# A gated FFN on one NeuronCore: the up projection by Strassen's seven block products, and the down projection as a phase of its own

## The chip, the cores and the metric

One Trainium2 chip, of which the kernel uses one core. A core has five engines that run their own instruction queues: TensorE (PE, matrix products into PSUM), VectorE (DVE), ScalarE (ACT), GpSimd (POOL) and SyncE (SP, which here issues every DMA). PSUM has eight banks, and a product tile of 128 rows by 512 f32 columns fills one of them. The metric is the device time of one execution in microseconds.

## The reference, cut to what matters

The kernel is one layer of a decoder: a mixer of four branches, and behind it a gated FFN with a short causal convolution. Only the FFN and its neighbours are touched here. The width is 1024, the sequence 1024 tokens, `D_FF` is 2816, and everything is f32.

```
h = rmsnorm(x, ffn_pre_g) * (1.0 + sc2) + sh2
u = causal_dwconv(h @ w_up, ffn_conv_w, ffn_conv_b)   # 1024 -> 5632, 3 taps
gate, val = split(u, 2)
y = (silu(gate) * val) @ w_down                       # 2816 -> 1024
x = x + g2 * rmsnorm(y, ffn_post_g)
```

(The body of the FFN is written out here in one piece.)

## The kernel before, in words

A product in nearly full f32 precision is made of three fast products. Each operand is split into a high part (the value cast to the rounded f32 type, "hi") and a low part (the value less the high part, "lo"), and PE multiplies hi by hi, hi by lo and lo by hi. `split_w` (L179 and below) does this for a weight tile of 128 by 1024: a DMA into a raw buffer (`wr`, two buffers), the cast on ACT (L184), the subtraction on POOL (L185).

Tokens are worked on in two halves of 512. The loop over eight token tiles `t` ahead of the FFN (from L957) does the output projection of the mixer (`yps`, L968), two RMS norms, and the transposes `h2t` (L989) that turn the normed tile to channels by tokens. ACT applies scale and shift (L991), and DVE makes hi and lo (`h2h`, `h2l`, L994 and L995) for each half.

The FFN works through 22 blocks `j` of 128 gate channels and the 128 value channels that belong to them. `up(j)` loads two weight tiles (gate and value), and for each makes 48 matmuls: two token halves, eight blocks of 128 input channels, three products (L1017). ACT and DVE do the convolution straight from PSUM (L1021, L1022, L1024), then silu, gate times value (L1028), and hi and lo of the activations (L1031, L1032), which stay in SBUF. `down` takes a group of two blocks, one group behind: for each of eight token tiles 12 matmuls per block into a PSUM tile (L1047), which DVE adds to an accumulator `ya` in SBUF (L1052). So up and down products alternate on PE all through the FFN. The last group is followed by the final norm (`rstd_of`, L249 to L255), the factor `grow1` on POOL (L1060), the sum with `x1l` (L1063) and the stores.

The order of the instructions on each engine is set by a scheduler that reorders the rows within the limits of data and buffers; it is not the order of the source.

Of the kernel before, what the change touches and what calls it, by code (L numbers as in the profile page):

```python
# [10 lines left out]
F32 = mybir.dt.float32  # L11
# [11 lines left out]
S = 1024  # L23
D = 1024
# [88 lines left out]
def tile_hybrid_block(ctx, tc, x, pos, ada, pk, cst, w_in, w_br, w_out, w_up, w_dn, out):  # L113
# [47 lines left out]
    sg_s = dram.tile([32, P, S], F32, name="sg_s")  # L161
    o_s = dram.tile([8, P, S], F32, name="o_s")
    x1_s = dram.tile([NT, P, D], F32, name="x1_s")
    QK = {}

    def qkslot(n, i):
# [90 lines left out]
    pss = ctx.enter_context(pool("pss", 2, PSUM))  # L257
# [6 lines left out]
    hi_pri = ExitStack()  # L264
    mrg = ExitStack()
    wox = ExitStack()
    h2H = [None] * 2
    h2L = [None] * 2
    with ExitStack() as mix:
        hp = mix.enter_context(pool("hp", 1))  # L270
        gx = mix.enter_context(ExitStack())
# [658 lines left out]
                        (G if br else V).tensor_tensor(out=accs[c], in0=accs[c], in1=sg, op=OP.add)  # L930


    big = ctx.enter_context(pool("big", 4))
    with pool("mg", 2) as mgp, pool("sms", 8) as sms, wox:
        wo = {}

# [14 lines left out]
        with pool("tmp", 7, side="right") as tmp, pool("grp", 1, side="right") as grp:  # L951
            for kp in range(4):
                load_wo(1, kp, obp, V if kp % 2 else G)
            grow0 = grp.tile([P, D], F32, name="grow0")
            spread_row(grow0, Gm, ptt, "t", tmp, "t")
            for t in range(NT):
# [25 lines left out]
                if t % 4 == 0:  # L982
                    h2H[half] = big.tile([P, NK, 512], F32R, name="h2h", tag="b")
                    h2L[half] = big.tile([P, NK, 512], F32R, name="h2l", tag="b")
                hf32 = jk.rearrange("p (a b) -> p a b", b=P)
# [7 lines left out]
                hd, ld = h2H[half][:, :, tl], h2L[half][:, :, tl]  # L993
                V.tensor_copy(hd, hf32)  # L994
                V.tensor_tensor(out=ld, in0=hf32, in1=hd.bitcast(F32), op=OP.subtract)  # L995


    psx.close()
    with pool("yac", 1) as yac, pool("act", 8) as actp, pool("wd", 6) as wdp, pool("ut", 5) as ut, \
            pool("sme", 8) as sme, pool("pd", 2, PSUM) as pd:  # L1000
        ya = [yac.tile([P, D], F32, name=f"ya{t}") for t in range(NT)]
        GRP = 2
        groups = [list(range(g, g + GRP)) for g in range(0, NF - 4, GRP)] + [[NF - 4], list(range(NF - 3, NF))]

        def up(j):
            us = []
            for v in range(2):
                m = j + v * NF
                hi, lo = split_w(w_up[m])
                ps = pss.tile([P, S], F32, name="ups", tag="s")  # L1010
                for hf in range(2):
                    n = 0
                    for k in range(NK):
                        ks = slice(k * P, (k + 1) * P)
                        xh, xl = h2H[hf][:, k, :], h2L[hf][:, k, :]
                        for a, b in ((hi, xh), (hi, xl), (lo, xh)):
                            PE.matmul(ps[:, hf * 512:hf * 512 + 512], a[:, ks], b, start=(n == 0), stop=(n == 23))  # L1017
                            n += 1
                u = ut.tile([P, S], F32, name="u", tag="u")
# [4 lines left out]
                V.scalar_tensor_tensor(out=u[:, 2:], in0=ps[:, 0:S - 2], scalar=w(0), in1=u[:, 2:],  # L1024
                                       op0=OP.mult, op1=OP.add)
# [3 lines left out]
            hi = actp.tile([P, S], F32R, name="ah", tag="a")  # L1029
            lo = actp.tile([P, S], F32R, name="al", tag="a")  # L1030
            A.copy(hi, us[0])  # L1031
            V.tensor_tensor(out=lo, in0=us[0], in1=hi.bitcast(F32), op=OP.subtract)  # L1032
            return hi, lo

        def down(gi, acts):
            ws = [split_w(w_dn[j], wdp) for j in groups[gi]]
            last = gi == len(groups) - 1
            for t in range(NT):
                tb = slice(t * P, (t + 1) * P)
                ps = pd.tile([P, D], F32, name="dps", tag="d")  # L1040
                n = 0
                tot = 3 * len(ws)
                for (ah, al), (wh, wl) in zip(acts, ws):
                    for a, b in ((ah, wh), (ah, wl), (al, wh)):
                        for hf in range(2):
                            cs = slice(hf * 512, hf * 512 + 512)
                            PE.matmul(ps[:, cs], a[:, tb], b[:, cs], start=(n == 0), stop=(n == tot - 1))  # L1047
                        n += 1
# [4 lines left out]
                if last:  # L1053
                    sm = sme.tile([P, 8], F32, name="sm4", tag="sm")
                    jk = ut.tile([P, D], F32, name="jk2", tag="u")
                    A.activation(jk, ya[t], AF.Square, accum_out=sm[:, 0:1])
                    rstd_of(sm[:, 0:1], sm)
                    x1 = ut.tile([P, D], F32, name="x1l", tag="u")
                    dma(x1, x1_s[t])
                    G.tensor_tensor(out=ya[t], in0=ya[t], in1=grow1, op=OP.mult)  # L1060
                    for hf in range(2):
                        cs = slice(hf * 512, hf * 512 + 512)
                        V.scalar_tensor_tensor(out=x1[:, cs], in0=ya[t][:, cs], scalar=sm[:, 3:4], in1=x1[:, cs],  # L1063
                                               op0=OP.mult, op1=OP.add)
                        dma(out[tb, cs], x1[:, cs])

        grow1 = yac.tile([P, D], F32, name="grow1")
        pend = None
        for gi in range(len(groups)):
            if gi == len(groups) - 1:  # L1070
                spread_row(grow1, Gf, pd, "d", ut, "u")
            acts = [up(j) for j in groups[gi]]
            if pend is not None:
                down(*pend)
            pend = (gi, acts)
        down(*pend)
    return dict(qk_s=qk_s, o_s=o_s, sg_s=sg_s, x1_s=x1_s, A2=A2, B2=B2)


# [68 lines left out]
```

## Time and profile before

| | |
|---|---|
| median of three runs | 2039.09 us (2036.22 to 2039.84) |
| profiled execution, its own time | 2032.69 us |
| its span | 2030.9 us |
| granted TensorE clock over the span | 0.962 |
| PE busy | 1855.4 us, 91% |
| DVE, ACT, POOL busy | 57%, 41%, 23% |
| up matmuls (L1017), three groups of 704 | 2112 |
| down matmuls (L1047), three groups of 352 | 1056 |

The span runs from the first to the last instruction of the profiled execution, and times inside it are counted from its start. The FFN takes its last 755 us: the first up matmul starts at 1275.48. A matmul's listed duration (about 390 ns) overlaps with the next one's; what one costs is the distance from start to start.

### The profile page before, as it was taken

How to read it: one execution, taken by the hardware profiler on the slowest of the kernel's cores; microseconds unless marked ns; L12 is line 12 of the kernel's file. 1: busy time of each engine (PE TensorE's matmuls, PEld its weight loads, DVE VectorE, ACT ScalarE, POOL GpSimd, SP SyncE). 2: the span in 40 equal slices, each digit the busy share in tenths (PEclk: the TensorE clock that was granted, in tenths of full speed). 3: DMA queues.
4: the chain of work that ended last, by engine and by line, in shares of the span. 5: the costliest groups of instructions: out<-in, count | busy, mean ns of one | idle time of the engine just before them, and what ended most of it. 6: DMA issues, size and time to landing. Idle time of an engine off the chain costs nothing. (4 is left out here: it accounts for less than half of the span.)

```text
span 2030.9 us, 22858 instructions
## 1 busy us (share of the span) xinstructions
PE 1855.4 (91%) x8792; PEld 1443.3 (71%) x8792; DVE 1154.4 (57%) x1731; ACT 829.5 (41%) x1458; POOL 472.9 (23%) x244
## 2 busy tenths in 40 slices
PE   6888877499999999899999899999999999999996
PEld 3655555376767776677787668788888888888875
DVE  6759999605899857685113765532343334433457
ACT  5556666236545645463222444333122212221122
POOL 0102145272111110011205610222122212222024
PEclk9988989699999999899999999999999999999999
DMA  8364423444514242513113632121111101111114
GB/s 312 94 165 151 174 84 93 126 92 104 187 57 125 78 129 69 147 42 115 62 63 129 225 122 83 63 73 42 32 63 58 47 32 52 62 52 42 32 62 145
DMA packets 61038, 197.30 MB, mean 97 GB/s; under 512 B 9153, under 2 KB 9281, under 8 KB 60929
## 3 DMA queue, kind: packets, MB, share of 16 engines
q1 hardware_dynamic: 60928, 195.84, 30.6%
q8 instruction: 69, 1.13, 0.2%
q14 instruction: 41, 0.33, 0.1%
HBM read 154.13 MB, written 41.68 MB: 96 GB/s over the span
## 5 line engine op out<-in xcount | busy, mean ns | idle before, releaser
L185 POOL TENSOR_TENSOR wlo<-wraw,whi 128x1024 fp32r<-128x1024 f32 x126 | 317.4, 2521 | 1384.2 <-ACT whi L184 1348.2
L365 PE MATMUL mm<-hH,whi 128*128 128x512 f32 x864 | 353.5, 409 | 49.6 <-ACT whi L184 31.5
L365 PE MATMUL mm<-hH,wlo 128*128 128x512 f32 x864 | 350.4, 406 | 3.7 <-POOL wlo L185 3.7
L365 PE MATMUL mm<-hL,whi 128*128 128x512 f32 x864 | 351.9, 407 | 0.9 <-DVE hL L321 0.9
L184 ACT CAST whi<-wraw 128x1024 fp32r<-128x1024 f32 x144 | 150.6, 1049 | 413.2 <-PE ups L1017 283.7
L1017 PE MATMUL ups<-h2h,whi 128*128 128x512 f32 x704 | 277.6, 395 | 1.3 <-DVE h2h L994 1.3
L1017 PE MATMUL ups<-h2l,whi 128*128 128x512 f32 x704 | 277.5, 394 | 0.5 <-DVE h2l L995 0.5
L1017 PE MATMUL ups<-h2h,wlo 128*128 128x512 f32 x704 | 274.5, 390 | 0.0
L1022 DVE SCALAR_TENSOR_TENSOR u<-ups,pkt,u 128x1023 f32<-128x1023 f32 x44 | 56.4, 1283 | 350.8 <-ACT u L1021 350.8
L365 PEld LDWEIGHTS mm<-hH,whi 128*128 128x128 f32 x864 | 166.6, 193 | 95.6 <-ACT whi L184 32.0
L365 PEld LDWEIGHTS mm<-hH,wlo 128*128 128x128 f32 x864 | 166.5, 193 | 41.4 <-POOL wlo L185 4.8
L365 PEld LDWEIGHTS mm<-hL,whi 128*128 128x128 f32 x864 | 167.2, 194 | 36.1 <-issue 2.6
L1017 PEld LDWEIGHTS ups<-h2h,whi 128*128 128x128 f32 x704 | 132.6, 188 | 32.3 <-DVE h2h L994 1.7
L1017 PEld LDWEIGHTS ups<-h2h,wlo 128*128 128x128 f32 x704 | 132.5, 188 | 29.8
L1017 PEld LDWEIGHTS ups<-h2l,whi 128*128 128x128 f32 x704 | 132.7, 189 | 28.2 <-DVE h2l L995 1.0
L1052 DVE TENSOR_TENSOR ya<-ya,dps 128x1024 f32<-128x1024 f32 x80 | 97.3, 1217 | 58.8 <-PE dps L1047 58.6
L605 DVE TENSOR_SCALAR_CACHE_REDUCE junkb<-key,cf 128x1024 bf16<-128x1024 uint16 (+3 forms) x124 | 117.3, 946 | 4.3
L1047 PE MATMUL dps<-whi,ah 128*128 128x512 f32 x352 | 109.4, 392 | 5.5 <-DVE ya L1052 5.5
L1047 PE MATMUL dps<-wlo,ah 128*128 128x512 f32 x352 | 108.6, 390 | 0.0
L1047 PE MATMUL dps<-whi,al 128*128 128x512 f32 x352 | 108.4, 389 | 0.0
L872 DVE SCALAR_TENSOR_TENSOR hc<-hpad,pkt,hc 128x1024 f32<-128x1024 f32 x60 | 84.2, 1408 | 0.0
L1047 PEld LDWEIGHTS dps<-whi,ah 128*128 128x128 f32 x352 | 65.4, 188 | 22.2 <-DVE ya L1052 8.9
(560 smaller groups left out, 2950.3 us busy)
## 6 DMA issues: line engine op xcount, KB each, us to landing
wraw<-in_w_in SPq DMA_DIRECT2D x54, 512.0 KB, 3.9
adaw<-in_ada SPq DMA_DIRECT2D x48, 512.0 KB, 5.9
wraw<-in_w_up SPq DMA_DIRECT2D x44, 512.0 KB, 3.3
sg_s<-gt SPq DMA_DIRECT2D x44, 256.0 KB, 2.6
sgl<-sg_s SPq DMA_DIRECT2D x22, 512.0 KB, 3.4
wraw<-in_w_dn SPq DMA_DIRECT2D x22, 512.0 KB, 3.3
xt<-in_x SPq DMA_DIRECT2D x16, 512.0 KB, 4.9
qis<-qk_s SPq DMA_DIRECT2D x16, 256.0 KB, 4.2
```

Source lines behind the costliest of these rows:

```text
L184: A.copy(hi, raw)
L185: (E or G).tensor_tensor(out=lo, in0=raw, in1=hi.bitcast(F32), op=OP.subtract)
L365: PE.matmul(ps, a[:, ks], b[:, k, cs], start=(n == 0), stop=(n == 3 * NK - 1))
L605: V.tensor_scalar(out=j[:, :n], in0=src, scalar1=scal, scalar2=None, op0=op, op1=OP.add, accum_out=dst[:, kc(t):kc(t) + 1])
L872: V.scalar_tensor_tensor(out=hc, in0=hpad[:, k:k + S], scalar=w(k), in1=hc, op0=OP.mult, op1=OP.add)
L1017: PE.matmul(ps[:, hf * 512:hf * 512 + 512], a[:, ks], b, start=(n == 0), stop=(n == 23))
L1022: V.scalar_tensor_tensor(out=u[:, 1:], in0=ps[:, 0:S - 1], scalar=w(1), in1=u[:, 1:], op0=OP.mult, op1=OP.add)
L1047: PE.matmul(ps[:, cs], a[:, tb], b[:, cs], start=(n == 0), stop=(n == tot - 1))
L1052: V.tensor_tensor(out=ya[t], in0=ya[t], in1=ps, op=OP.add)
```

## The change

The up product of a block `j` is seen as a 2 by 2 block product. The rows are gate (1) and value (2), the inner dimension is cut into channels 0 to 511 (1) and 512 to 1023 (2), and the tokens into the two halves. In place of eight block products the new code makes seven, in the form due to Winograd, from sums and differences of weight blocks (`s1` to `s4`, made for every `j`) and of input blocks (`t1` to `t4`, made once). Each of the seven (`product`) is 12 matmuls of 128 by 512, in one PSUM bank, 84 per `j` in place of 96.

`prep(j)` makes the weight operands: two raw loads (`wr1` gate, `wr2` value, in the same two raw buffers), two sums on DVE (`wsum`), two differences on POOL, and seven splits, each a cast on ACT and a subtraction on POOL. `split_t` does the same once for the input blocks. The seven products are put together on DVE by seven additions per `j` (`add`), each of a PSUM bank and an SBUF tile, into one SBUF buffer `ub`. `conv(j)` then reads `ub`, no longer PSUM, and stores the activation to a scratch `act_s` in DRAM.

The down projection comes when all 22 blocks are done. It loads the activations back and splits them again, loads every block of `w_dn` twice (once per token half), sums over all 22 blocks in PSUM in four tiles of two banks, and ends each token tile from PSUM. The accumulator `ya` and its additions are gone. The first half of the normed input passes through a scratch `hf_s`, and `grow1` is made ahead of the FFN and kept in the scratch `grow_s`.

```diff
+        def prep(j):
+            r1 = wr.tile([P, D], F32, name="wr1", tag="w")
+            r2 = wr.tile([P, D], F32, name="wr2", tag="w")
+            dma(r1, w_up[j])
+            dma(r2, w_up[j + NF])
+            sf = wsp.tile([P, 3, 512], F32, name="wsum", tag="s")
+            def split(wpool, r):
+                b = wpool.tile([P, 2, 512], F32R, name="wblk", tag="w")
+                A.copy(b[:, 0], r)
+                G.tensor_tensor(out=b[:, 1], in0=r, in1=b[:, 0].bitcast(F32), op=OP.subtract)
+                return b[:, 0], b[:, 1]
+            w["a11"] = split(wp, r1[:, c0])
+            tt(V, sf[:, 0], r2[:, c0], r2[:, c1], OP.add)
+            tt(V, sf[:, 1], sf[:, 0], r1[:, c0], OP.subtract)
+            w["s2"] = split(wp, sf[:, 1])
+            w["s1"] = split(wp, sf[:, 0])
+            w["a12"] = split(wb, r1[:, c1])
+            tt(G, r2[:, c0], r1[:, c0], r2[:, c0], OP.subtract)
+            w["s3"] = split(wb, r2[:, c0])
+            tt(G, sf[:, 2], r1[:, c1], sf[:, 1], OP.subtract)
+            w["s4"] = split(wb, sf[:, 2])
+            w["a22"] = split(wb, r2[:, c1])
...
+        for k in range(4):
+            t2 = ptp.tile([P, 512], F32, name="t2", tag="p")
+            V.tensor_tensor(out=t2, in0=f1[:, 4 + k], in1=f0[:, k], op=OP.subtract)
+            split_t("t2", k, t2)
+            G.tensor_tensor(out=f0[:, 4 + k], in0=f0[:, 4 + k], in1=t2, op=OP.subtract)
...
+                u = ub[:, 2 + v]
-                A.activation(u, ps, AF.Identity, bias=pc("fb", m, m + 1), scale=w(2))
-                V.scalar_tensor_tensor(out=u[:, 1:], in0=ps[:, 0:S - 1], scalar=w(1), in1=u[:, 1:],
+                A.activation(u, c, AF.Identity, bias=pc("fb", m, m + 1), scale=w(2))
+                V.scalar_tensor_tensor(out=u[:, 1:], in0=c[:, 0:S - 1], scalar=w(1), in1=u[:, 1:],
                                        op0=OP.mult, op1=OP.add)
...
             V.tensor_tensor(out=us[0], in0=us[0], in1=us[1], op=OP.mult)
+            dma(act_s[j], us[0])
...
+        for j in range(NF):
+            if 2 <= j + 1 < NF:
+                prep(j + 1)
+            p1 = p1s.pop(j)
+            add(u2, product(j, "s2", "t2"), p1)
+            p5 = product(j, "s1", "t1")
+            add(u4, p5, u2)
+            if j > 1:
+                second(j)
+            add(cg[:, c0], p2s.pop(j), p1)
+            add(u3, product(j, "s3", "t3"), u2)
+            add(cv[:, c1], p5, u3)
+            add(cg[:, c1], product(j, "s4", "b22"), u4)
+            if 2 <= j + 1 < NF:
+                first(j + 1)
+            add(cv[:, c0], product(j, "a22", "t4"), u3)
+            conv(j)
...
-                if gi == 0:
-                    A.copy(ya[t], ps)
-                else:
-                    V.tensor_tensor(out=ya[t], in0=ya[t], in1=ps, op=OP.add)
```

**Where the rows stand.** First PE at the start of the up projection. The names are the output and inputs of each row: `h2t` the transposes of a token tile, `yps` the projection ahead of the FFN, `ups` the up products. Before, up matmuls surround the transposes of the last two token tiles:

```order
L1017 MATMUL ups<-h2h,whi 128x512
L1017 MATMUL ups<-h2l,whi 128x512
L989 MATMUL h2t<-ctile,xt_9864 128x128 x8
L1017 MATMUL ups<-h2h,wlo 128x512
L1017 MATMUL ups<-h2h,whi 128x512
L1017 MATMUL ups<-h2l,whi 128x512
```

After, the same place on PE:

```order
L999 MATMUL h2t<-ctile,xt_9890 128x128 x8
L974 MATMUL yps<-whi,mhi 128x512
L974 MATMUL yps<-wlo,mhi 128x512
L974 MATMUL yps<-whi,mlo 128x512
L974 MATMUL yps<-whi,mhi 128x512
L974 MATMUL yps<-wlo,mhi 128x512
L974 MATMUL yps<-whi,mlo 128x512
L999 MATMUL h2t<-ctile,xt_9982 128x128 x8
L1061 MATMUL ups<-h2h,wblk 128x512
L1061 MATMUL ups<-h2l,wblk 128x512
```

The first up product now stands behind the transposes of the last token tile.

Second, DVE in the middle of the up projection. Before, one block `j` (`u` is a convolution buffer, `al` the activations' low part):

```order
L1022 SCALAR_TENSOR_TENSOR u_11129<-ups_11080,pkt_60,u_11129 128x1023
L1024 SCALAR_TENSOR_TENSOR u_11129<-ups_11080,pkt_60,u_11129 128x1022
L1022 SCALAR_TENSOR_TENSOR u_11188<-ups_11139,pkt_60,u_11188 128x1023
L1024 SCALAR_TENSOR_TENSOR u_11188<-ups_11139,pkt_60,u_11188 128x1022
L1028 TENSOR_TENSOR u_11129<-u_11129,u_11188 128x1024
L1032 TENSOR_TENSOR al_11195<-u_11129,ah_11194 128x1024
```

After, one round from the two sums of `prep(j+2)` to the end of `conv(j)`; four more additions from PSUM follow before the next round's first row:

```order
L1039 TENSOR_TENSOR wsum_11056<-wr2_11053 128x512
L1039 TENSOR_TENSOR wsum_11056<-wsum_11056,wr1_11052 128x512
L1125 TENSOR_TENSOR ub_10270<-ups_11000,u4_10941 128x512
L1115 SCALAR_TENSOR_TENSOR ub_10270<-ub_10270,pkt_60 128x1023
L1117 SCALAR_TENSOR_TENSOR ub_10270<-ub_10270,pkt_60 128x1022
L1125 TENSOR_TENSOR ub_10270<-ups_11029,u3_10942 128x512
L1115 SCALAR_TENSOR_TENSOR ub_10270<-ub_10270,pkt_60 128x1023
L1125 TENSOR_TENSOR u2_11082<-ups_11085,p1_11027 128x512
L1117 SCALAR_TENSOR_TENSOR ub_10270<-ub_10270,pkt_60 128x1022
L1121 TENSOR_TENSOR ub_10270<-ub_10270 128x1024
```

The four convolution steps (L1115, L1117) read two SBUF operands where they read one from PSUM before, and the two weight sums stand at the head of the round.

Third, POOL. Before it had two splits of 128 by 1024 for each `j` in the up projection. After, this is one round, the same as DVE's above, from the low part of `a22` of the block before (in `wr2_10911`) on:

```order
L1036 TENSOR_TENSOR wblk_10937<-wr2_10911,wblk_10937 128x512
L1036 TENSOR_TENSOR wblk_11068<-wr1_11052,wblk_11068 128x512
L1039 TENSOR_TENSOR wr2_11053<-wr1_11052,wr2_11053 128x512
L1039 TENSOR_TENSOR wsum_11056<-wr1_11052,wsum_11056 128x512
L1036 TENSOR_TENSOR wblk_11072<-wr2_11053,wblk_11072 128x512
L1036 TENSOR_TENSOR wblk_11062<-wsum_11056,wblk_11062 128x512
L1036 TENSOR_TENSOR wblk_11076<-wsum_11056,wblk_11076 128x512
L1036 TENSOR_TENSOR wblk_11065<-wsum_11056,wblk_11065 128x512
```

Then come the low part of the next block's `a11`, and that of this block's `a22`, which ends the round. The raw buffer of `wr2` is free only when that last row is done, and the next load into it is queued on SP behind the store of `conv(j)`'s activation.

## Rows read from the trace of the kernel before

**Rows 1.** Busy time of each engine by stretch, in us (instructions in brackets)

```profile
core 0: us, PE busy (x) PEld busy (x) DVE busy (x) ACT busy (x) POOL busy (x), PEclk, DMA share, GB/s
1300.00:1900.00 600.00, 600.00 (x2628) 493.10 (x2627) 231.41 (x186) 151.19 (x143) 134.94 (x56) 1.00 0.15 50
```

**Rows 2.** The page's costliest groups: busy us, mean ns of one, idle before

```profile
L1017 PE MATMUL ups<-h2h,whi 128*128 128x512 f32 x704 | 277.6, 395 | 1.3 <-DVE h2h L994 1.3
...
L1052 DVE TENSOR_TENSOR ya<-ya,dps 128x1024 f32<-128x1024 f32 x80 | 97.3, 1217 | 58.8 <-PE dps L1047 58.6
...
L1047 PE MATMUL dps<-whi,ah 128*128 128x512 f32 x352 | 109.4, 392 | 5.5 <-DVE ya L1052 5.5
```

**Rows 3.** Source lines: duration in ns, minimum/median/maximum, first and last start

```profile
L407 POOL TENSOR_TENSOR sw<-r,rhi x12: 1262/1294/1302, 309.2 to 484.2; 128x512 fp32r<-128x512 f32 x12
L948 DVE TENSOR_TENSOR mlo<-macc,mhi x16: 674/676/2462, 1151.6 to 1187.2; 128x512 fp32r<-128x512 f32 x16
L400 DVE TENSOR_TENSOR r<-mm,cosinv x4: 681/690/692, 67.9 to 83.6; 128x512 f32<-128x512 f32 x4
L872 DVE SCALAR_TENSOR_TENSOR hc<-hpad,pkt,hc x60: 1248/1269/3448, 525.6 to 680.5; 128x1024 f32<-128x1024 f32 x60
L1028 DVE TENSOR_TENSOR u<-u x19: 1216/1225/2791, 1311.0 to 1881.7; 128x1024 f32<-128x1024 f32 x19
L947 ACT CAST mhi<-macc x16: 612/617/624, 1150.6 to 1184.1; 128x512 fp32r<-128x512 f32 x16
L1021 ACT ACTIVATE u<-ups,pkt x44: 1187/1202/1209, 1300.9 to 1964.4; 128x1024 f32<-128x1024 f32 x44
L1027 ACT ACTIVATE u<-u x22: 1058/1062/1062, 1306.2 to 1957.4; 128x1024 f32<-128x1024 f32 x22
```

**Rows 4.** The page's DMA issues: count, KB each, us from issue to landing

```profile
wraw<-in_w_up SPq DMA_DIRECT2D x44, 512.0 KB, 3.3
```

**Rows 5.** Timeline of DVE and POOL: start us, duration us, idle before

```profile
1149.30 1.22 DVE L930 TENSOR_TENSOR macc<-macc,sgl 128x1024 f32<-128x1024 f32 x1
1150.44 1.22 DVE L928 TENSOR_TENSOR sgl<-brp,sgl 128x1024 f32<-128x1024 f32 x1
1151.58 1.78 DVE L948 TENSOR_TENSOR mlo<-macc,mhi 128x512 fp32r<-128x512 f32 x1
1153.28 3.40 DVE L930 TENSOR_TENSOR macc<-macc,sgl 128x1024 f32<-128x1024 f32 x1
...
1149.87 5.72 POOL L185 TENSOR_TENSOR wlo<-wraw,whi 128x1024 fp32r<-128x1024 f32 x2 [5.89 <-ACT whi L184]
```

**Rows 6.** Timeline where the up projection starts

```profile
1275.48 0.40 PE L1017 MATMUL ups<-h2h,whi 128*128 128x512 f32 x1
...
1287.32 1.06 PE L989 MATMUL h2t<-ctile,xt 128*128 128x128 f32 x8 [0.19 <-DVE xt L981]
...
1288.05 2.90 ACT L991 ACTIVATE jk<-h2t,B,A 128x128 f32<-128x128 f32 x8 [2.49 <-PE h2t L989]
```

**Rows 7.** Timeline of the end: last matmuls, and DVE behind them

```profile
2015.51 0.61 PE L1047 MATMUL dps<-whi,al 128*128 128x512 f32 x2
...
2024.03 1.78 DVE L252 SCALAR_TENSOR_TENSOR sm<-sm 128x1 f32<-128x1 f32 x1
...
2026.27 1.41 DVE L1063 SCALAR_TENSOR_TENSOR x1l<-ya,sm,x1l 128x512 f32<-128x512 f32 x2
```

**Rows 8.** PE's timeline behind a wait

```profile
1184.25 0.50 PE L968 MATMUL yps<-whi,mhi 128*128 128x512 f32 x1 [2.69 <-ACT mhi L947]
...
1188.34 0.63 PE L968 MATMUL yps<-wlo,mhi 128*128 128x512 f32 x1
1188.77 0.63 PE L968 MATMUL yps<-whi,mlo 128*128 128x512 f32 x1
...
1191.63 0.39 PE L968 MATMUL yps<-whi,mhi 128*128 128x512 f32 x1
1191.86 1.88 PE L244 MATMUL row<-diag,ones 128*128 128x512 f32 x4
```

More of the change, by code (lines that the diff above doesn't have):

```diff
@@ L163, in tile_hybrid_block @@
     x1_s = dram.tile([NT, P, D], F32, name="x1_s")
+    hf_s = dram.tile([P, NK, 512], F32, name="hf_s")
+    act_s = dram.tile([NF, P, S], F32, name="act_s")
+    grow_s = dram.tile([P, D], F32, name="grow_s")
     QK = {}
@@ L266, in tile_hybrid_block @@
     wox = ExitStack()
-    h2H = [None] * 2
-    h2L = [None] * 2
     with ExitStack() as mix:
@@ L992, in tile_hybrid_block @@
                                      bias=B2[:, j0 + j:j0 + j + 1])
-                hd, ld = h2H[half][:, :, tl], h2L[half][:, :, tl]
-                V.tensor_copy(hd, hf32)
-                V.tensor_tensor(out=ld, in0=hf32, in1=hd.bitcast(F32), op=OP.subtract)
-    psx.close()
[L999 to L1005, printed above, removed]
+                if half == 0:
+                    hd, ld = h2H[:, :, tl], h2L[:, :, tl]
+                    dma(hf_s[:, :, tl], hf32)
+                    V.tensor_copy(hd, hf32)
+                    V.tensor_tensor(out=ld, in0=hf32, in1=hd.bitcast(F32), op=OP.subtract)
+                else:
+                    k0, k1 = slice(0, 4), slice(4, 8)
+                    a0, a1 = f0, f1
+                    E = V if t == NT - 1 else G
+                    E.tensor_tensor(out=a0[:, k0, tl], in0=a1[:, k0, tl], in1=a0[:, k0, tl], op=OP.subtract)
+                    G.tensor_tensor(out=a1[:, k0, tl], in0=a1[:, k1, tl], in1=a1[:, k0, tl], op=OP.subtract)
@@ L1006, in up @@
             us = []
-            for v in range(2):
+            for v, c in ((0, cg), (1, cv)):
                 m = j + v * NF
[L1009 to L1019, printed above, removed]
+                u = ub[:, 2 + v]
@@ new lines, in acts @@
+        def acts(j, half, rp, hp_, tag):
+            raw = rp.tile([P, 512], F32, name="actw", tag=tag)
+            dma(raw, act_s[j][:, half * 512:half * 512 + 512])
+            hi = hp_.tile([P, 512], F32R, name="acth", tag=tag)
+            lo = hp_.tile([P, 512], F32R, name="actl", tag=tag)
+            A.copy(hi, raw)
+            V.tensor_tensor(out=lo, in0=raw, in1=hi.bitcast(F32), op=OP.subtract)
+            return hi, lo
+        CH = [[0, 1]] + [list(range(j, j + 4)) for j in range(2, 14, 4)] + [list(range(14, 18)), list(range(18, NF))]
@@ new lines, in tile_hybrid_block, with down @@
+        early = [(acts(j, 0, ptp, ptp, "p"), split_w(w_dn[j])) for j in CH[0]]
+        upx.close()
+        pd = ctx.enter_context(pool("pd", 4, PSUM))
+        yps = [pd.tile([P, D], F32, name="dps", tag="d") for t in range(4)]
+        def down(chunk, ops, tl, ps, hfs):
+            for hfg in hfs:
+                for n, ((ah, al), (wh_, wl_)) in enumerate(ops):
+                    for i, (a, b) in enumerate(((ah, wh_), (ah, wl_), (al, wh_))):
+                        for hf in hfg:
+                            cs = slice(hf * 512, hf * 512 + 512)
+                            PE.matmul(ps[:, cs], a[:, tl], b[:, cs], start=(chunk == 0 and n == 0 and i == 0),
+                                      stop=(chunk == len(CH) - 1 and n == len(ops) - 1 and i == 2))
@@ new lines, in tile_hybrid_block @@
+        for t in range(4):
+            down(0, early, slice(t * P, t * P + P), yps[t], ((0, 1),))
+    bigx.close()
+    with pool("wdn", 20) as wdn, pool("adn", 20) as adn, pool("adr", 4) as adr, pool("dt", 5) as dtp, pool("grq", 1) as grq, \
+            pool("sme", 8) as sme:
+        grow1 = grq.tile([P, D], F32, name="grow1")
+        dma(grow1, grow_s)
+        for half in range(2):
+            for ci, ch in enumerate(CH):
+                if half == 0 and ci == 0:
+                    continue
+                ops = [(acts(j, half, adr, adn, "p"), split_w(w_dn[j], wdn)) for j in ch]
+                if ci == 0:
+                    yps = [pd.tile([P, D], F32, name="dps", tag="d") for t in range(4)]
+                for t in range(4):
+                    tg = 4 * half + t
+                    fin = tg == NT - 1 and ci == len(CH) - 1
+                    down(ci, ops, slice(t * P, t * P + P), yps[t], ((0,), (1,)) if fin else ((0, 1),))
+                    if ci < len(CH) - 1:
+                        continue
+                    tb = slice(tg * P, (tg + 1) * P)
+                    ps = yps[t]
+                    sm = sme.tile([P, 8], F32, name="sm4", tag="sm")
+                    jk = dtp.tile([P, D], F32, name="jk2", tag="u")
+                    yg = dtp.tile([P, D], F32, name="yg", tag="u")
+                    x1 = dtp.tile([P, D], F32, name="x1l", tag="u")
+                    dma(x1, x1_s[tg])
+                    hs = (slice(0, 512), slice(512, 1024)) if fin else (slice(0, D),)
+                    for i, cs in enumerate(hs):
+                        A.activation(jk[:, cs], ps[:, cs], AF.Square, accum_out=sm[:, 5 + i:6 + i])
+                        V.tensor_tensor(out=yg[:, cs], in0=ps[:, cs], in1=grow1[:, cs], op=OP.mult)
+                    if fin:
+                        V.tensor_tensor(out=sm[:, 5:6], in0=sm[:, 5:6], in1=sm[:, 6:7], op=OP.add)
+                    rstd_of(sm[:, 5:6], sm)
@@ L1068, in tile_hybrid_block @@
[L1068 to L1076, printed above, removed]
     return dict(qk_s=qk_s, o_s=o_s, sg_s=sg_s, x1_s=x1_s, A2=A2, B2=B2)
```

104 lines of the change are left out of this document (71 added, 33 removed).

## The prediction

> **What bounds the kernel now.** I read the stretches first. From 1300 to 1900 us PE is busy for all of 600 us at a granted clock of 1.00, with 2628 matmuls [rows 1], so one 128x512 matmul costs 600 / 2628 = 0.228 us from start to start. No other engine is busy for 40% of that stretch. The groups then say what PE waits for: next to nothing in the up matmuls, 5.5 us of `ya` in one of the three down groups [rows 2]. So matmuls are what the FFN costs. The source lines give the price of each operation that the change multiplies [rows 3], and the timelines show the start [rows 6] and the end [rows 7]. The reader is to see one thing more, in the timeline of DVE and POOL [rows 5], on which the forecast rests.
>
> There DVE and POOL work side by side. DVE's first row (two SBUF operands) runs to 1150.52. POOL's first subtraction, issued at 1149.87, has not ended before DVE's third row can start: a 128x512 subtraction of two SBUF operands that takes 0.68 us by its median takes 1.78. Then the next one, 1.21 us of work, takes 3.40, and the two POOL splits of 2.4 us each take 5.72 together. Worked out, the four take turns: POOL 1150.5 to 1152.7, DVE to 1153.3, POOL to 1155.5, DVE to 1156.7. The row between, L928 with an operand in PSUM, keeps its 1.22 although POOL is running. So a DVE operation with two SBUF operands and a POOL operation don't overlap, and whoever waits goes next. The maxima agree: 2.46 over 0.68 for L948, 3.45 over 1.27 for L872, 2.79 over 1.22 for L1028 [rows 3].
>
> The Trainium skill says the same ("SBUF — State Buffer", section "Who interferes with whom"): a VectorE instruction with two SBUF inputs and a GpSimd instruction that reads SBUF lock each other out for the whole instruction, one with an input in PSUM is free of it. The trace agrees, with 1.78 us for 0.68 and with 1.22 for the PSUM row. By the page's rule the rounds below are long; without it they would be hidden under PE, and the sum would be that of the first rival.
>
> **The matmuls.** Up falls from 2112 to 22 x 84 = 1848, so 264 x 0.228 = 60.2 us are saved on PE. Down keeps 1056. A block `j` now costs PE 84 x 0.228 = 19.2 us.
>
> **The round of preparing weights.** Per `j` POOL has nine operations of 128x512 at 1.29 us [rows 3], 11.6 us. DVE has seven additions from PSUM (0.69 each, free of POOL) and, with two SBUF operands, two weight sums at 0.68, four convolution steps priced by L872 at 1.27, and the product at 1.22 [rows 3]: 7.7 us. What cannot overlap is thus 19.3 us per `j`, already as much as PE's 19.2. And it cannot be spread over the round. The order rows show why: the next `wr2` load needs the raw buffer that POOL's low part of `a22` frees, and stands on SP behind the activation's store, so behind DVE's product; and DVE's convolution stands behind the next round's weight sums. So the load is a hole, in which POOL has one operation to do and DVE none of the seven. The round is at least the load, 3.3 us [rows 4], plus the sums 1.4, plus eight POOL operations 10.3, plus four convolution steps and product 6.3: **21.3 us**.
>
> Walked through with turns, from the end of `a22`'s low part: load to 3.4; sums to 4.8; POOL makes `s3`, `s4` and the low part of `s3` to 8.6 (ACT has cast `s3` and done the gate's first step by 7.9: 0.62 and 1.20 [rows 3]); convolution step to 9.9; POOL `s2` to 11.2; step to 12.5; silu and the cast of `s4`, 1.06 and 0.62 on ACT, to 14.2, where neither has work; POOL `s4` to 15.5; step to 16.8; POOL `s1` to 18.1; step to 19.3; POOL next `a11` to 20.6; product to 21.9; POOL `a22` to **23.2**. This leaves out handing on from engine to engine; I add 0.5 by choice and take 23.7, with 21.3 and 25 as bounds. PE's 19.2 is then hidden under the round, with 4.5 us of waiting. The PSUM additions are hidden in POOL's turns; there are eight banks, so PE isn't held by them. If the turns weren't, the round would be 16.9 by the same walk, below PE.
>
> **The start.** Before, up matmuls begin at 1275.5 and fill the gaps around the last transposes; now they stand behind them. Those run at 1287.3 as before (their chain is on DVE and ACT, not in the FFN), and ACT ends the scaled tile at 1290.95 [rows 6]. From there to the low part of `a22` of the third block (`j` = 2) the program's rows count 32 POOL operations (41.3 us), 22 two-operand DVE subtractions and sums (15.0 us), and one convolution step, 1.3 us, since the input blocks `t1` to `t4` and three blocks' weights all come here. That is 57.6 us that can't overlap, to 1348.6; with two short holes I take **1350**. If they did overlap it would be 1332, and with each load a hole 1360.
>
> **To the end.** From `j` = 2 to 21 there are 19 more rounds: 19 x 23.7 = 450.3, to 1800. When the last `a22` is split PE has some four products of 2.74 left: 10 us more (by the walk, as `s1` comes 5 us before it). Early down products wait for the last bank's addition, a load of activations (priced as 3.3, although half the size), cast and low part: 0.7 + 3.3 + 0.6 + 0.7, so 6 us in round numbers; 0 if SP gets there early, 15 if the down weights' splits on POOL (2.4 us each) queue up. Down itself: 1056 x 0.228 = 240.8; its loads and splits per block (one POOL split, one cast of 1024 and one of 512, one small DVE subtraction) are below the 5.5 us of its 24 matmuls, and 20 buffers run ahead. Half to half, where PSUM tiles pass on: 2 us (0 to 5). The additions to `ya` (97.3 us of DVE [rows 2]) lay under PE but for the waits at the very end.
>
> **The tail.** Before, the last matmul ends at 2016.1 and the span at 2030.9: 14.8 us. DVE's last rows show one reason: a one-column operation of 1.78 us [rows 7], which I put down to POOL's product of that time (L1060), as above. POOL has no work here now, and the tile is finished in two halves. My estimates: square and sum of half a tile 0.8 (ACT's 1.06 for 1024 [rows 3], halved, and a read), product 0.7, small steps 1.7 (six one-column rows of 0.15 to 0.2 [rows 7] and their hand-overs), two steps of 1.41 together [rows 7], and from the end of the last step (2027.68 [rows 7]) to the span's end 3.2 as before: 7.8, taken as 7.9 us. Bounds 6 and 11.
>
> **Sum.** 1350 + 450.3 + 10 + 6 + 240.8 + 2 + 7.9 = 2067, against the span of 2030.9: 36 us more. The profiled execution's own time is 1.8 above its span, and the median of the runs 6.4 above that; I carry the difference to the median: 2039.1 + 36 = **2075**. The saving of 60 us on PE is real, but PE waits.
>
> **Rivals.** 0.2% of the time, 4 us, is about what a measurement can tell from no change.
> - **PE stays the bound: faster.** The new convolution steps or POOL's half-size operations might not lock, so that rounds of 16.9 hide. For it: the timeline shows L930, L948 and L185 [rows 5], not this mix. Against: L872, the same operation, has the long maximum. The start is then about 1340 for the last input block, with 72 of the 1848 matmuls done: 1340 + 1776 x 0.228 + 6 + 240.8 + 2 + 7.9 = 2002, or **2010** for the median. It decides at 21.8 us per round: below, the kernel gets faster.
> - **Rounds at their floor.** If POOL's and DVE's operations are queued so well that no hole is left but the load, 19 x 21.3 = 405, and the median is **2030**: slightly faster, or no change.
> - **The clock falls too.** Behind a wait of 2.69 us, matmuls start 0.43 us apart at 1188.3, twice the 0.23 to which they are back at 1191.6 [rows 8]: the lower of the two levels (1.2 in place of 2.4 GHz), for 7 us. One such wait per round costs 3.3 us (16 matmuls at 0.43 less 0.228), which fits into the 4.5 of waiting. Two would cost 6.6, and make rounds of 25.8: **2115**.
> - **The change doesn't do what it says:** nothing for it; the rows have 84 matmuls per `j`.
>
> **Chances.** Rounds of 22.4 to 25 us 0.66 (own range 2050 to 2100); floor 0.12; PE bound 0.12; clock 0.10. Faster: 0.12 and a third of the floor, 0.16; same 0.05; slower 0.79. The range leaves out the PE bound and part of the clock case: 2024 to 2112.
>
> **What would show it.** In the up phase: PE busy about 80%, starts of like matmuls of neighbouring blocks 23 to 24 us apart; convolution steps and the product on DVE of 2 us and more where 1.27 and 1.22 are their work; POOL above 1.29 in its mean; PE waiting for POOL's `wblk`. Last `a22` near 1800. In down, PE full at 1.00. Wrong if convolution steps keep 1.27 with POOL busy, or PE is full in the up phase; if PE's matmuls lie 0.43 apart for most of it, the last rival holds.

## The result, and the profile after

The changed kernel takes 2050.78 us in the median of four runs (2049.8 to 2052.79), the one before 2037.68 (2036.22 to 2039.84). The ratio is 1.0065, with an interval of 1.0047 to 1.0082. So it is slower, as forecast, but by 13 us and not by 36. Between the profiled executions the difference is 20.1 us (spans of 2051.0 and 2030.9); both comparisons are used below, and the sum of the prediction is a span. The two differ because one execution of each kernel was profiled: the one before took 2032.69 us, 5.0 below its median, the changed one 2052.79, 2.0 above its own.

The page of the changed kernel, two of its groups: busy us, mean ns of one, idle before and what ended it.

```profile
L1036 POOL TENSOR_TENSOR wblk<-wr,wblk 128x512 fp32r<-128x512 f32 x88 | 152.4, 1751 | 1.2 <-ACT wblk L1035 1.2
L1061 PE MATMUL ups<-h2h,wblk 128*128 128x512 f32 x352 | 126.8, 424 | 24.5 <-DVE ub L1125 20.5
```

POOL's subtraction of 1.29 us [rows 3] now has a mean of 1.75. PE's wait of 20.5 us is put down to DVE's addition, which reads a product's PSUM bank and so frees it; it is not a wait for POOL's `wblk`, as I had named it. It also contradicts "there are eight banks, so PE isn't held by them": the additions stand in DVE's order behind the convolution steps and the product, so a bank comes free late although eight were there.

Stretches of the changed kernel, columns as in [rows 1]: the start of up, and 200 us in its middle.

```profile
1280.00:1350.00 70.00, 40.58 (x137) 29.20 (x136) 45.30 (x49) 31.18 (x63) 52.88 (x36) 0.76 0.12 42
1400.00:1500.00 100.00, 98.07 (x431) 80.23 (x430) 67.70 (x66) 32.94 (x48) 70.09 (x43) 1.00 0.23 79
1500.00:1600.00 100.00, 91.30 (x381) 71.95 (x380) 69.05 (x66) 34.95 (x51) 69.11 (x42) 0.97 0.21 73
```

PE is full until about 1487, since it still has the blocks prepared during the start to work off; then it waits in every round, for about 2 us in most and 0.4 to 0.9 in the others. In the first stretch it is idle for 29 of 70 us and its clock is 0.76.

Source lines of the changed kernel: ns, minimum/median/maximum. L1115 and L1117 are the convolution's two steps, L1121 the product of gate and value, L1125 the additions from PSUM.

```profile
L1115 DVE SCALAR_TENSOR_TENSOR ub<-ub,pkt x44: 1279/1287/1770, 1350.4 to 1798.9; 128x1023 f32<-128x1023 f32 x44
L1117 DVE SCALAR_TENSOR_TENSOR ub<-ub,pkt x44: 1270/1734/2801, 1352.6 to 1800.2; 128x1022 f32<-128x1022 f32 x44
L1121 DVE TENSOR_TENSOR ub<-ub x22: 1219/2202/2210, 1358.8 to 1802.0; 128x1024 f32<-128x1024 f32 x22
L1125 DVE TENSOR_TENSOR ub<-ups,u x66: 673/683/693, 1347.7 to 1796.5; 128x512 f32<-128x512 f32 x66
```

The long durations are all with two SBUF operands; those with an operand in PSUM never exceed 0.70. L1115 has a median of 1.29: in the round shown further down the value's first step starts just before POOL ends an operation (1503.95), and then POOL's next one is the one that is long (1.90).

One round on the chain of waits of the changed kernel (start, us, what):

```profile
1489.02 3.24 DMA wr<-in_w_up
...
1492.70 0.70 DVE wsum L1039
...
1493.53 1.76 POOL wr L1039
...
1497.11 1.77 DVE ub L1115
1498.90 2.23 DVE ub L1117
...
1502.17 0.61 ACT wblk L1035
...
1502.85 1.30 POOL wblk L1036
...
1504.50 6.35 POOL wblk L1036 x3
1510.87 3.27 DMA wr<-in_w_up
```

It is the walk of the prediction, in its order: load, sums, POOL, convolution steps, the cast of `s4` behind the silu, four POOL subtractions (`s4`, `s1`, the next `a11`, `a22`), next load. It takes 21.85 us from load to load.

### The profile page after: what moved, and what is told of

Read it like the earlier page. It is cut to its first block, busy times and chain, and to the rows that moved or that the text cites. A ratio compares the mean times of both kernels' runs of the same rounds, so it can differ in the third digit from the quotient of the medians.

```text
span 2051.0 us, 23324 instructions
## 1 busy us (share of the span) xinstructions
PE 1825.2 (89%) x8528; PEld 1407.1 (69%) x8528; DVE 1292.7 (63%) x1892; ACT 904.8 (44%) x1648; POOL 757.1 (37%) x429
## 5 line engine op out<-in xcount | busy, mean ns | idle before, releaser
L1061 PE MATMUL ups<-th,wblk 128*128 128x512 f32 x1320 | 314.6, 394 | 16.6 <-POOL th L1086 8.0
L1061 PEld LDWEIGHTS ups<-th,wblk 128*128 128x128 f32 x1320 | 248.0, 189 | 77.3 <-POOL th L1086 9.2
L1036 POOL TENSOR_TENSOR wblk<-wr,wblk 128x512 fp32r<-128x512 f32 x88 | 152.4, 1751 | 1.2 <-ACT wblk L1035 1.2
L1061 PE MATMUL ups<-h2h,wblk 128*128 128x512 f32 x352 | 126.8, 424 | 24.5 <-DVE ub L1125 20.5
L1036 POOL TENSOR_TENSOR wblk<-wsum,wblk 128x512 fp32r<-128x512 f32 x66 | 111.5, 1692 | 68.9 <-ACT wblk L1035 68.9
L1115 DVE SCALAR_TENSOR_TENSOR ub<-ub,pkt 128x1023 f32<-128x1023 f32 x44 | 66.2, 1505 | 92.6 <-ACT ub L1114 92.6
L1168 PE MATMUL dps<-whi,acth 128*128 128x512 f32 x352 | 110.5, 393 | 11.2 <-ACT acth L1152 10.2
L1168 PE MATMUL dps<-wlo,acth 128*128 128x512 f32 x352 | 111.2, 395 | 1.7 <-POOL wlo L188 1.7
L1168 PE MATMUL dps<-whi,actl 128*128 128x512 f32 x352 | 110.4, 393 | 0.2 <-DVE actl L1153 0.2
L1061 PEld LDWEIGHTS ups<-h2h,wblk 128*128 128x128 f32 x352 | 71.7, 204 | 47.5 <-DVE ub L1125 26.5
L1117 DVE SCALAR_TENSOR_TENSOR ub<-ub,pkt 128x1022 f32<-128x1022 f32 x44 | 84.5, 1921 | 0.7
```

Source lines behind the costliest of these rows:

```text
L1036: G.tensor_tensor(out=b[:, 1], in0=r, in1=b[:, 0].bitcast(F32), op=OP.subtract)
L1061: PE.matmul(ps, u[:, ks], v[:, k, :], start=(n == 0), stop=(n == 11))
L1115: V.scalar_tensor_tensor(out=u[:, 1:], in0=c[:, 0:S - 1], scalar=w(1), in1=u[:, 1:], op0=OP.mult, op1=OP.add)
L1117: V.scalar_tensor_tensor(out=u[:, 2:], in0=c[:, 0:S - 2], scalar=w(0), in1=u[:, 2:], op0=OP.mult, op1=OP.add)
L1168: PE.matmul(ps[:, cs], a[:, tl], b[:, cs], start=(chunk == 0 and n == 0 and i == 0), stop=(chunk == len(CH) - 1 and n == len(ops) - 1 and ...
```

## The experiments

Each has its ratio to the kernel before, run beside it. Experiments 1 to 4, 5 to 8 and 9 to 12 ran on three different chips, on which the kernel before had medians of 2035.55, 2034.47 and 2032.46 us. So kernels are compared by their ratios; a difference of ratios is turned into us with 2037.68. "Raw tiles" are the tiles into which a block's weights are loaded (`wr`). The code cuts are shortened to the lines that matter.

**1. The convolution's input in PSUM.** The output blocks `cg` and `cv` are PSUM tiles; products have four banks.

```
-    px = upx.enter_context(pool("px", 8, PSUM))
+    px = upx.enter_context(pool("px", 4, PSUM))
+    pcx = upx.enter_context(pool("pcx", 1, PSUM))
...
-        cg, cv = ub[:, 0], ub[:, 1]
+        cg = pcx.tile([P, S], F32, name="cg")
+        cv = pcx.tile([P, S], F32, name="cv")
```

> The assembled gate and value rows (cg, cv) lie in PSUM in place of SBUF; the products keep four banks in place of eight; the work and the output are the same. Theory A (DVE operations with two SBUF operands and POOL operations exclude each other): the four convolution steps, 5.1 us per round, no longer take turns with POOL, POOL's low parts of s2, s1, a11 and a22 come back to about 1.3 us in place of 1.9, the step L1117 to 1.28 in place of 1.7 to 2.2, and the round falls from 21.8 to PE's 19.2 to 19.9, so the span from 2051 to about 2005 to 2015. Theory B (the round is the chain of load, casts and hand-overs, and the turns cost nothing that the chain wouldn't): the round stays at 21.3 to 21.8 and the span within 10 us of 2051. If four banks are too few, PE waits for DVE and the span is above 2051.

Measured: 2011.7 us, 0.9894 (0.9877 to 0.991). Source lines of this kernel, and its weight sums on DVE ten rounds apart:

```profile
L1119 DVE SCALAR_TENSOR_TENSOR ub<-cg,pkt,ub x22: 1271/1281/1284, 1347.4 to 1751.0; 128x1022 f32<-128x1022 f32 x22
L1119 DVE SCALAR_TENSOR_TENSOR ub<-cv,pkt,ub x22: 1271/1275/1282, 1350.5 to 1754.1; 128x1022 f32<-128x1022 f32 x22
```

```profile
1512.98 0.69 DVE L1040 TENSOR_TENSOR wsum<-wr 128x512 f32<-128x512 f32 x1 [3.00 <-DMA wr<-in_w_up]
...
1711.07 0.69 DVE L1040 TENSOR_TENSOR wsum<-wr 128x512 f32<-128x512 f32 x1 [2.56 <-DMA wr<-in_w_up]
```

The second step (L1119 here), which had a median of 1.73 and a maximum of 2.80, now never exceeds 1.29, though it does the same work beside the same POOL. Rounds fall to 19.8 (1512.98 to 1711.07). The exclusion is shown: one operand in PSUM ends it. Only the four steps are freed: the weight sums and the product keep two SBUF operands and their turns (the product at 1506.17 takes 1.87). That the products have four banks doesn't hold PE by itself: experiment 6 has four, too, and PE is full.

**2. Only the gate's half in PSUM** (`cv` stays in SBUF, `px` has six banks).

> Only the gate row (cg) lies in PSUM; the products keep six banks. Theory A: the two steps of the gate, 2.5 us of the round's locked time, are free, those of the value still take turns: the round falls by 1.2 to 2 us, to 19.8 to 20.6, the span to 2013 to 2028. Theory B: no change within 10 us.

Measured: 2028.81 us, 0.9968 (0.9954 to 0.9982). In one kernel, the same line with both kinds of operand:

```profile
L1119 DVE SCALAR_TENSOR_TENSOR ub<-cg,pkt,ub x22: 1273/1282/1283, 1346.8 to 1768.9; 128x1022 f32<-128x1022 f32 x22
L1119 DVE SCALAR_TENSOR_TENSOR ub<-ub,pkt x22: 1274/1726/2814, 1350.0 to 1772.0; 128x1022 f32<-128x1022 f32 x22
```

Only the SBUF half is long, and the round lies between those of the changed kernel and of experiment 1 (20.0 to 22.5 from 1375 on, 20.7 on average).

**3. A third raw tile**, so that the next `wr2` needn't wait for POOL's `a22`.

```
-    ... pool("pt", 6) as ptp:
+    ... pool("pt", 5) as ptp, pool("wx", 1) as wx:
...
-            r2 = wr.tile([P, D], F32, name="wr2", tag="w")
+            r2 = (wr if j < 2 or j % 2 else wx).tile([P, D], F32, name="wr2", tag="w")
```

> A third raw weight buffer, so that the load of wr2 no longer waits for the low part of a22 of the block before (the pool of temporaries has five buffers in place of six to make room); the lock stays. Theory A and B both have the load's 3.3 us in the round: without it A gives the port's own sum, about 18.5 to 20 by turns, so PE's 19.2 or a little above, span 2005 to 2025; B gives 18.5, so PE's 19.2. If the round stays at 21.8, the load is not part of it, and the buffer was not what held it.

Measured: 2004.31 us, 0.9856 (0.9839 to 0.9873). PE of this kernel by stretch, and DVE's weight sums in two early rounds:

```profile
1400.00:1700.00 300.00, 300.00 (x1320) 247.48 (x1319) 209.88 (x220) 129.36 (x174) 215.65 (x143) 1.00 0.24 83
```

```profile
1393.78 0.68 DVE L1039 TENSOR_TENSOR wsum<-wr 128x512 f32<-128x512 f32 x1
...
1411.84 0.68 DVE L1039 TENSOR_TENSOR wsum<-wr 128x512 f32<-128x512 f32 x1
```

PE is full at 1.00, in rounds of 19.12, although the second convolution step keeps its median of 1.73. While PE still worked off the start's blocks, the preparation alone went in rounds of 18.06. This run bears on the step that failed: the work that I listed as exclusive, 19.3 us, fits into 18.06 with the exclusion in force.

**4. The new down projection alone**, behind the up projection of before (2112 matmuls), which stores its activations.

> The other half of the change alone: the up projection as before, with 96 matmuls per block straight from PSUM to the convolution, activations stored to the scratch, and the new down phase. Up from 1275.5 with 2112 x 0.228 = 481.5 to 1757, then a few us of transition (3 to 10), down 241, tail 9: span 2010 to 2017, 14 to 21 us less than before. If the down phase as such costs time (its loads, the half change), it is at or above 2031.

Measured: 2029.2 us, 0.9967 (0.9954 to 0.9979). From 1300 to 1750 PE is full. The new down phase as such gives 7 us by the ratio and 4 between the profiles, not the span of 2010 to 2017 that I expected. In the profile part of the rest is at the step between the phases, where PE works 16.3 of the 20 us from 1780, and part ahead of up, whose last transposes end some 6 us later; I have not separated them further.

**5. One POOL subtraction more per round** (the low part of `a22` made twice).

> The changed kernel with one POOL operation more per round: the low part of a22 is computed twice, before its raw buffer is given back. No gain is meant; it prices one turn. Theory A: the round is a chain of turns with no slack, and each block is 1.2 to 1.3 us longer, 21.8 to 23.0 or 23.1, the span 23 to 26 us more than 2051. If the chain had slack on POOL (POOL is busy only 70% of the stretch), the span would move by less than 8 us.

Measured: 2061.8 us, 1.0133 (1.0113 to 1.0153): by the ratios 14 us more than the changed kernel, between the profiles 10.6, in place of 23 to 26. This doesn't price a turn: the scheduler also put rows in another order (the low part of `s3` ahead of the difference for `s4`, and an addition between the two weight sums). Inconclusive.

**6. Experiments 1 and 3 together.**

> Both cures together: the third raw buffer (e3) and the assembled rows in PSUM (e1). Theory A: e3's rounds are PE's own 19.12 us, so taking the turns away as well brings nothing in the rounds, and the time is that of e3 within 5 us; the last turns at the end of the up projection and four banks can shift it by a few us either way. If locked turns still cost something in e3, it is 8 us or more below it.

Measured: 2011.58 us, 0.9882 (0.9853 to 0.991), with PE at 300.00 of 300 in rounds of 19.12, as in 3. Once PE is the bound, a shorter preparation buys nothing. By the ratio it is 5 us above 3, but the intervals overlap, and its four runs alone spread over 12 us (2002.6 to 2014.75). The profiled one is the slowest of them; its last transposes come at 1298.00, in 3 at 1291.11.

**7. The third raw tile from the second block on** (`wx if j % 2 else wr`).

> As e3, but the third buffer takes the odd blocks' wr2, the second block's (j = 1) among them, so that its load need not wait until POOL has split all of the first block. DVE sat idle for 12.5 us there, with the input blocks' first differences queued behind the sum that needs this load. Theory A: the start is limited by turns, 57 us of work that can't overlap from 1291 on; DVE's part starts 10 us earlier, into the time when POOL works alone, and then takes turns: 3 to 7 us less than e3. If the start were bound by this load alone, 10 to 12 us less. No change if POOL's own queue is what the products wait for.

Measured: 2001.48 us, 0.9841 (0.9819 to 0.9862): the fastest here by its median, though its interval overlaps those of 3, 6, 8, 11 and 12.

**8. Kernel 7 with the twenty input-block splits off POOL**: ACT copies each block into PSUM, so that DVE's subtraction doesn't exclude POOL.

```
+    px = upx.enter_context(pool("px", 6, PSUM))
+    pst = upx.enter_context(pool("pst", 2, PSUM))
...
+            cp = pst.tile([P, 512], F32, name="cp", tag="c")
+            A.copy(cp, src)
+            V.tensor_tensor(out=th[b][:, 4 + k], in0=cp, in1=th[b][:, k].bitcast(F32), op=OP.subtract)
```

> As e7, and the 20 splits of the input blocks read a copy in PSUM that ACT makes (two banks, six left for products), all on DVE: one SBUF operand each, so no turns with POOL, and six POOL operations fewer. Theory A: of the 57 us at the start that can't overlap, 14 subtractions on DVE (9.5) and 6 on POOL (7.7) go: 8 to 15 us less than e7, or less if ACT, which gets 12 us more work, is then the limit (0.6 per copy). Without a lock at the start only the six operations on POOL go, and ACT's extra work makes it 0 to 5 us either way.

Measured: 2001.93 us, 0.9837 (0.9817 to 0.9858): nothing against 7. ACT's timeline in this kernel points to a reason:

```profile
1340.49 0.58 ACT L1088 COPY cp<-hf 128x512 f32<-128x512 f32 x1
1341.01 0.62 ACT L1085 CAST th<-hf 128x512 fp32r<-128x512 f32 x1
```

It copies and casts without a gap from 1331 to 1342, and PE waits 6.92 us for its cast, until 1338.56. So a wait for ACT has taken the place of one for POOL (5.98 us in 7); experiment 12 shows that ACT isn't the only bound.

**9. One POOL subtraction less** (the low part of `s1` left out, its high part used twice).

> The changed kernel without the subtraction that makes the low part of s1 (its product uses the high part twice, so the output is not the reference's): one POOL operation less per round, the other rows in the same order. Theory A (a chain of turns): one turn of 1.1 us less, round 21.8 to about 20.7, span 18 to 25 us below 2051. If POOL's idle time of 30% were slack, no change within 6 us.

Measured: 2046.33 us, 1.0058 (1.004 to 1.0077): by the ratio 1 us less than the changed kernel, well inside both intervals, where 18 to 25 were expected; rounds stay at 21.7. The chain of waits of this kernel has another way round:

```profile
1482.90 2.21 DVE ub L1123
1485.13 0.33 SPq L123
...
1485.55 4.18 DMA wr<-in_w_up
```

The load now waits on SP for the store of the activation, and so for DVE's product (L1123 here) in place of POOL's `a22`. The next product starts at 1505.00, 22.1 us later. So the round has two chains of nearly one length (in the changed kernel the product ends at 1509.72, 1.15 us ahead of the load that waits for `a22`), and shortening POOL's alone gives nothing. It is no price of a turn either.

**10. The product of gate and value left out** (the value row is stored in its place).

> The changed kernel without the product of gate and value on DVE (the value row is stored in its place, so the output is not the reference's): one DVE operation of 1.22 us with two SBUF operands less per round, other rows in the same order. Theory A: the low part of a22 no longer waits for its turn, 1.1 us less, round about 20.7, span 18 to 25 us below 2051, although DVE is idle for 30% of the round. If only POOL's own work counts, no change within 6 us.

Measured: 2025.98 us, 0.9963 (0.9948 to 0.9978): by the ratio 21 us below the changed kernel, as expected. From 1376 on the weight sums go in rounds of 20.4 to 21.1 but for one of 22.1 and one of 21.7, a turn of DVE less; it shortens both chains of experiment 9.

**11. Kernel 7 with six banks for products in place of eight.**

> As e7 with six PSUM banks for products in place of eight. In the runs with fewer banks (e1, e2, e6, e8) the first product ran before the last token tile's transposes, from 1280 to 1287 on, in e3 and e7 behind them, because the first product's bank was one that the output projection still held. Expected: the first product starts some 8 us before the last transposes, but what follows waits for POOL and for the input blocks as before, so the time is that of e7 within 4 us. If PE's idle time there were on the path, 5 to 8 us less.

Measured: 2006.26 us, 0.9871 (0.9855 to 0.9888), by the ratio 6 us above 7, with intervals that just overlap; rounds are 19.12 again. So with a third raw tile two banks fewer cost PE nothing in the rounds.

**12. Kernel 7 with every second input-block split as in 8, the others on POOL.**

> As e8, but only every second split of the input blocks goes through a copy in PSUM to DVE (ten), the other ten go to POOL from SBUF as they are. ACT has ten copies less, 5 us, and was the limit in e8 (25 us of casts and copies back to back); POOL has 10 more operations of 1.25 in time in which it was idle for 14 us, and no DVE operation with two SBUF operands to take turns with. Expected: the last input block 3 to 6 us earlier than in e8, the time 3 to 6 us below e7 and e8. No gain if prep of the third block, behind these splits on ACT and POOL, is what PE waits for next.

Measured: 2002.86 us, 0.9852 (0.9838 to 0.9867): nothing again, though ACT has ten copies less than in 8. From the last transposes to the end of the span are 708.3 us in 7, 706.8 in 8 and 708.8 here: the start stays as it is with all three ways of sharing it out.

## Why the prediction was right in its direction and wrong in its size

**The step that failed is the size of the round**, 23.7 us in "19 x 23.7 = 450.3". The third block's `a22` ends its low part at 1355.4 (forecast 1350), the last block's at 1770.4: 19 rounds of 21.84, 415.0 us in place of 450.3. POOL and DVE in that round of the changed kernel, start and duration:

```profile
1503.95 1.28 DVE L1115 SCALAR_TENSOR_TENSOR ub<-ub,pkt 128x1023 f32<-128x1023 f32 x1 [2.24 <-ACT ub L1114]
1505.16 0.68 DVE L1125 TENSOR_TENSOR u<-ups,p 128x512 f32<-128x512 f32 x1
1505.76 1.73 DVE L1117 SCALAR_TENSOR_TENSOR ub<-ub,pkt 128x1022 f32<-128x1022 f32 x1
1507.52 2.20 DVE L1121 TENSOR_TENSOR ub<-ub 128x1024 f32<-128x1024 f32 x1
```

```profile
1504.50 1.90 POOL L1036 TENSOR_TENSOR wblk<-wsum,wblk 128x512 fp32r<-128x512 f32 x1 [0.35 <-ACT wblk L1035]
1506.37 5.73 POOL L1036 TENSOR_TENSOR wblk<-wr,wblk 128x512 fp32r<-128x512 f32 x3
```

From 1503.95 to 1512.10 (1506.37 + 5.73) lie three DVE operations and four of POOL that exclude each other. By their undisturbed durations they are 1.28 + 1.27 + 1.22 + 4 x 1.29 = 8.93 us; they took 8.15. That is 0.78 less over six changes from one to the next, 0.13 each. I priced each turn at its full listed duration. Nearly half of the 0.13 has nothing to do with turns: listed durations overlap on one engine as well. Where DVE is idle, POOL's operations of 1.29 start 1.25 apart (1300.70 and 1301.95, shown in the last section), and in [rows 5] DVE's of 1.22 start 1.14 apart (1149.30 and 1150.44). The row that I built on already said otherwise: in [rows 5] the four turns, with POOL's split at its median of 2.41, sum to 2.4 + 0.68 + 2.4 + 1.21 = 6.69 and run from 1150.52 to 1156.68, 6.16, again 0.13 per turn. From the sums to the load the walk has 19.8 us (3.4 to 23.2) and the round 18.17 (1492.70 to 1510.87), 1.63 less, of which the ten handovers in it make 1.3 if each is worth 0.13, an estimate from the rows above; the load with the way to the sums took 3.68 for 3.4. So the round is 21.85 for 23.2. The 0.5 that I added for handing on was wrong in sign. Together 1.86 x 19 = 35.3 us.

The same error stands in "what cannot overlap is thus 19.3 us per `j`, already as much as PE's 19.2": experiment 3 prepares a block in 18.06. So the exclusion alone doesn't hold PE up. It does so together with the load's hole. Either one taken away, the exclusion of the four convolution steps (experiment 1, 19.8) or the hole (experiment 3, 19.12), brings the round to PE's or near it; both together give no more (6). The Trainium skill ("SBUF — State Buffer", section "Who interferes with whom") has the two engines locked out for the whole instruction, with an operand in PSUM as the way out. Experiments 1 and 2 agree on the way out (1.28 against medians of 1.73); the turns here are 0.13 us shorter than the instructions listed.

**The other terms came out too small**, together by 19.3 us. The step to down of the changed kernel, PE's timeline:

```profile
1794.17 1.22 PE L1168 MATMUL dps<-whi,acth 128*128 128x512 f32 x2 [10.21 <-ACT acth L1152]
...
1796.04 1.05 PE L1168 MATMUL dps<-whi,actl 128*128 128x512 f32 x2
1796.89 1.05 PE L1168 MATMUL dps<-whi,acth 128*128 128x512 f32 x2
...
1799.87 0.62 PE L1168 MATMUL dps<-whi,acth 128*128 128x512 f32 x2
1800.33 0.63 PE L1168 MATMUL dps<-wlo,acth 128*128 128x512 f32 x2
```

- To the third block: 1355.4 for 1350. The last transposes came at 1295.37 where they came at 1287.32 before [rows 6], and ACT ended the scaled tile at 1299.40 for 1290.95. I had put them down as unchanged. From there to the third block's `a22` it took 56.0 us where I had 59, so the exclusive work of the start was priced too high as well.
- To the end of up: 13.6 us for 10. When the last `a22` was split PE had some 56 matmuls left, and not the 48 of four products, and waited 0.48 for a bank.
- To down: 10.2 us for 6. On the chain of waits the early load of activations starts at 1788.09, behind DVE's product of the last block but one and its store on SP, 4.1 us after up's last matmul where I had 0.7; it then took 5.39, where I took 3.3 from the larger weight loads.
- Down: 247.9 us for 242.8. Behind the wait of 10.21 two matmuls take 0.85 from start to start, then 0.46 from 1799.87 on: the lower level of the clock for 5.7 us; then PE waits 0.96 and 1.71 near 1811.
- Tail: 8.9 us for 7.9; the last matmul starts at 2041.67 and ends at 2042.06.

In sum: 2067 + 5.4 - 35.3 + 3.6 + 4.2 + 5.1 + 1.0 = 2051, the span. One more term lies behind the span: I carried 8.2 us from it to the median, since the profiled execution before was a quick one; the changed kernel's was the slowest of its four, and its span is 0.2 above their median. So of the 36 us that I forecast 20.1 are left between the spans, and 13.1 between the medians; the step from 20 to 13 comes from which executions were profiled.

**Right:** the forecast's mechanism. Two-operand DVE steps take turns with POOL, the load of the raw tile is a hole, and PE waits; the additions from PSUM stay out of it. **Rivals:** the floor (21.3 per round) is the one that came nearest in the rounds; it missed the end by the terms after the rounds, which were too small in it too. For the same reason the kernel isn't faster at 21.84, next to the 21.8 where I had the sign change. PE as the bound is what experiments 3 and 7 made of it: their ratios of 0.9856 and 0.9841 are next to that rival's, 2010 to 2039.1 or 0.986. The clock's fall in each round stayed small: 0.97 in the stretch from 1500, with waits of about 2 us.

**Signs that I named wrongly:** PE's share in up (80%) is 283.3 of 300 us, since PE first works off the start's blocks and since a round is shorter; and PE waits at DVE's additions (20.5 us), which stand in DVE's order between and behind the convolution steps, not at `wblk`. By its median only the second convolution step is long; the first keeps 1.29, which by "wrong if convolution steps keep 1.27 with POOL busy" would have counted against the forecast, although there it is POOL that takes the longer turn.

**Where the 60 us of saved matmuls went.** From the last transposes to the end of the span are 755.6 us; the 2904 matmuls at 0.228 and the tail are 671. Rounds longer than PE's account for 19 x 2.7 = 52, less what PE had in hand; experiment 7 removes 47 of the 85 that lie between (708.3 remain). The other 37 are the start, where PE waits 3.93, 7.83 and 3.21 us and its clock falls behind them (0.76 in the stretch), the step to down (10.2) and what down took above its matmuls (7.1). Experiments 8 and 12 didn't move them. What limits the start beside ACT in 8, and DVE with POOL in 7, stays open.

## What to carry to other kernels

Where two engines exclude each other, price a turn by the distance between starts in a row where they alternate, not by the sum of their undisturbed durations; over a round of ten turns this is put at 1.3 of the 1.86 us that the forecast was off. Look for the serial link in the round before shaving its work: a third raw tile made the preparation 3.8 us shorter per block, while one POOL subtraction less made it no shorter, since a second chain of the same length stood behind it. An operand in PSUM took a DVE operation out of the contention altogether.

## What the runs showed of the hardware that I had not expected

In the start DVE and POOL fall into step, and each pair of operations takes one pitch. POOL's timeline of the changed kernel, with DVE idle and then with DVE busy:

```profile
1300.70 1.29 POOL L1014 TENSOR_TENSOR hf<-hf 128x512 f32<-128x512 f32 x1
1301.95 1.30 POOL L1036 TENSOR_TENSOR wblk<-wr,wblk 128x512 fp32r<-128x512 f32 x1
...
1314.33 1.74 POOL L1039 TENSOR_TENSOR wsum<-wr,wsum 128x512 f32<-128x512 f32 x1
1316.03 1.73 POOL L1036 TENSOR_TENSOR wblk<-wr,wblk 128x512 fp32r<-128x512 f32 x1
```

There every POOL subtraction starts 1.70 us behind the last, with one DVE operation of 0.68 between: 1.29 + 0.68 would be 1.97, so 0.27 is saved per pair, 0.13 per handover as above. By the distances of the undisturbed engines, 1.25 and 0.60 (DVE's additions of 0.68 at 1487.78 and 1488.38), it would be 1.85, so the turns themselves save 0.15 of the 0.27. An output in SBUF doesn't bring the exclusion back: the steps of experiment 1 write to SBUF and read one SBUF operand, and keep 1.28.

The stage ahead of up, whose code no experiment but 4 changes, ends at other times from profile to profile: the last transposes start at 1287.32 before [rows 6], 1295.37 in the changed kernel, 1289.04 in experiment 7, 1298.00 in 6. Each is one execution, and experiment 6 alone spread over 12 us in its four runs, so this needn't be a property of the kernels. A forecast from one profile can't be held to better than that, and stretches are best compared from these transposes on.
